# Attention in a two-layer trunk: pairs of heads in a pipeline of quarter query projections, with ScalarE normalising the probabilities

## The chip, the core and the metric

The kernel runs on one core of one Trainium2 chip. A core has five engines that work side by side, each through a list of instructions of its own, in order: TensorE (PE, matrix products and transposes, with its weight loads shown apart as PEld), VectorE (DVE), ScalarE (ACT), GpSimd (POOL) and SyncE (SP, which issues the transfers from memory here). An instruction at the head of its list waits until semaphores say that its inputs are there and its output buffer is free, and what stands behind it on that engine waits with it. PE writes to a small memory of eight banks called PSUM, from which DVE and ACT read. The metric is the device time of one execution in microseconds (us); lower is better.

## The reference

The program is a decoder trunk of two layers on 256 tokens of width 1024. Each layer is a feed-forward half step (SwiGLU, 2816 wide), a mixer, and a second half step, with RMSNorm before and after each. The mixer of layer 0 is a pooling; that of layer 1 is attention with 8 heads of width 64 in each of three groups (windows 128, 512, 2048 at dilations 1, 4, 16). Only that attention is touched:

```python
q = apply_rope((h @ w_q).reshape(B, S, 3, 8, 64), cos, sin)
for g, (window, dilation) in enumerate(ATTN_GROUPS):
    s = einsum(q[g], k[g]) * 64 ** -0.5          # masked to the window, causal, dilated
    m = max(s); p = exp(s - m); den = sum(p)
    o[g] = einsum(p / den, v[g]); lse[g] = m + log(den)
o = sum_g softmax(lse)[g] * o[g]
return o.reshape(B, S, 512) @ w_o
```

Since the three groups are joined by their softmax denominators, a head is one softmax over the keys of all three groups: exp over all of them, one sum, one division, and one product with the stacked values. Both kernels compute it so.

## The kernel before

The tokens are sorted by residue, so that for a tile of 128 tokens a head needs 512 keys: 256 of group 0, 128 of group 1, 128 of group 2. There are two token tiles (i = 0, 1) and four pairs of heads (pr = 0 to 3; heads 2 pr and 2 pr + 1).

Weights come in units of 128x1024 numbers (128x768 for the queries) by SyncE's queue. ACT makes the high part of each unit (a CAST, L92 or L100) and DVE the low part (a subtraction, L93 or L101), and PE forms every projection as three products of high and low parts. A unit's converted copy sits in one of eight buffers. The attention stage begins when the values have been projected (`vp`). For each pair there is a query projection `qp` of 24 matmuls per tile from four units, `rope` on DVE (L499, two of L502, L503), three transposes `qtp` (L611) and a copy `qT` on ACT (L612).

`scores(i, hd)` is for one head: three products into a bank `sc` (64 rows of PE's array, since a head is 64 wide), mask and maximum on DVE (L551), a factor on the maximum (`nm`, L553), and exp with its sum on ACT (L554). `values(i, hd)` transposes the 128x512 probabilities on PE (`ptp`, L564), copies them to SBUF on ACT (`pTt`, L567), and multiplies: the transposed probabilities are the stationary operand and the 64 columns of a head's values stream through, into 64 columns of a bank `ob`. `normed` divides a tile's result by the sums on DVE (L581, L583), transposes it (`otp`, L591) and splits it into high and low parts (`oT`, L593, L594). `o_proj` multiplies it with the output weights into `acc_o`.

Then comes a boundary, the object `go`: `go.first` is the norm after the mixer with the residual sum (`jk_pm`, L152, on ACT; `y_m` and `h` on DVE; a power on POOL), `go.second` the norm before the next half step (`jk_qm`, `n_m`), `go.third` the transposes `tp_m` (L181) and their split into `aT_m` (L183, L184). The next half step starts with 96 matmuls into `acc_b` (tile 0, then tile 1) and goes on with the gate `g`.

The order on each engine is found by a scheduler, which sorts the instructions when the program is built by their place in the text, by when they can run, and by which buffers are free. It has put the conversions of a pair's query units ahead of the work that waits for them, and interleaved the heads' work of tile 0 and tile 1 with the projections.

Of the kernel before, what the change touches and what calls it, by code (L numbers as in the profile page):

```python
# [47 lines left out]
def trunk_kernel(ctx: ExitStack, tc: tile.TileContext, x, pos, gains, pscale, ws, wq, invf, amask, pmat, icnt, out):  # L48
    nc = tc.nc

    cp = ctx.enter_context(tc.tile_pool(name="cp", bufs=1))
# [5 lines left out]
    sc4 = ctx.enter_context(tc.tile_pool(name="sc4", bufs=2))  # L57
    sc2 = ctx.enter_context(tc.tile_pool(name="sc2", bufs=7))
# [23 lines left out]
    last = {}  # L82
# [13 lines left out]
    def load_q_unit(u):  # L96
        raw = rawp.tile([P, 1024], F32, tag="raw", name=f"rawq{u}")
        nc.sync.dma_start(raw[:, :768], wq[u])
        hl = hlp.tile([P, 2, 1024], F32R, tag="hl", name=f"hlq{u}")
        nc.scalar.copy(hl[:, 0, :768], raw[:, :768])  # L100
        nc.vector.tensor_sub(hl[:, 1, :768], raw[:, :768], hl[:, 0, :768])  # L101
        return hl

    def mm(o, l, r, start, stop):
        nc.tensor.matmul(o, l, r, start=start, stop=stop)  # L105
# [102 lines left out]
    def acc_pair(name):  # L208
        return [accp.tile([P, 512], F32, tag="acc", name=f"acc_{name}{k}") for k in range(2)]
# [284 lines left out]
    def rope(src, i, nh, name):  # L494
        r = sc2.tile([P, nh, 2, 32], F32, tag="w2", name=f"ra_{name}")
        b = sc2.tile([P, nh, 2, 32], F32, tag="w2", name=f"rb_{name}")
        s4 = src.rearrange("p (h two d) -> p h two d", two=2, d=32)
        c4 = ctab[:, i : i + 1].to_broadcast([P, nh, 2, 32])
        nc.vector.tensor_mul(r, s4, c4)  # L499
        for z in range(2):  # L500
            sz = stab[:, i, z : z + 1].to_broadcast([P, nh, 32])
            nc.vector.tensor_mul(b[:, :, z], s4[:, :, 1 - z], sz)  # L502
        nc.vector.tensor_add(r, r, b)  # L503
        return r.rearrange("p h two d -> p (h two d)")
# [28 lines left out]
    den = [cp.tile([P, 8], F32, name=f"den{i}") for i in range(2)]  # L533
    ob = {}
    npt = [0]

    probs = {}

    def scores(i, hd, pool, tag):

        pr, off = hd // 2, (hd % 2) * 64
        q = qT[pr // 2][:, pr % 2]
        sc = pool.tile([P, 512], F32, tag=tag, name=f"sc{i}_{hd}")
        t = slice(i * P, (i + 1) * P)
        a = slice(off, off + 64)
        mm(sc[:, 0:256], q[a, 0, t], kT[0][a, pr, :], True, True)
        mm(sc[:, 256:384], q[a, 1, t], kT[1][a, pr, t], True, True)
        mm(sc[:, 384:512], q[a, 2, t], kT[2][a, pr, t], True, True)
        p = sc2.tile([P, 512], F32, tag="w2", name=f"p{i}_{hd}")
        mx = st.tile([P, 1], F32, tag="mx", name=f"mx{i}_{hd}")  # L550
        nc.vector.tensor_tensor_reduce(p, sc, am[:, i], 1.0, -3.0e38, op0=ALU.add, op1=ALU.max, accum_out=mx)  # L551
        nm = st.tile([P, 1], F32, tag="nm", name=f"nm{i}_{hd}")
        nc.vector.tensor_scalar_mul(nm, mx, -0.125)  # L553
        nc.scalar.activation(p, p, AF.Exp, bias=nm, scale=0.125, accum_out=den[i][:, hd : hd + 1])  # L554
        probs[i, hd] = p

    def values(i, hd):
        part, at = (0, hd * 64) if i == 0 else (hd // 4, (hd % 4) * 64)
        if (i, part) not in ob:
            ob[i, part] = accp.tile([P, 512], F32, tag="acc", name=f"ob{i}{part}")  # L560
        p = probs.pop((i, hd))
        tp = tpp.tile([P, 4, P], F32, tag="tp", name=f"ptp{i}_{hd}")
        for c in range(4):
            nc.tensor.transpose(tp[:, c], p[:, c * P : (c + 1) * P], ident)  # L564
        pT = pTt[:, npt[0] % 4]
        npt[0] += 1
        nc.scalar.copy(pT, tp)  # L567
        o = ob[i, part][:, at : at + 64]
        n = slice(hd * 64, hd * 64 + 64)
        mm(o, pT[:, 0], vt[0][:, 0, n], True, False)  # L570
        mm(o, pT[:, 1], vt[0][:, 1, n], False, False)
        mm(o, pT[:, 2], vt[1][:, i, n], False, False)
        mm(o, pT[:, 3], vt[2][:, i, n], False, True)

    acc_f = [None, None]

    def normed(i, part, heads):

        n = heads // 2
        rd = st.tile([P, 8], F32, tag="rd", bufs=2, name=f"rd{i}{part}")  # L580
        nc.vector.reciprocal(rd[:, :heads], den[i][:, part * heads : part * heads + heads])  # L581
        on = sc2.tile([P, heads, 64], F32, tag="w2", name=f"on{i}{part}")
        nc.vector.tensor_mul(  # L583
            on,
            ob[i, part][:, : heads * 64].rearrange("p (h d) -> p h d", d=64),
            rd[:, :heads].unsqueeze(2).to_broadcast([P, heads, 64]),
        )
        tp = tpp.tile([P, 4, P], F32, tag="tp", name=f"otp{i}{part}")
        onf = on.rearrange("p h d -> p (h d)")
        for c in range(n):  # L590
            nc.tensor.transpose(tp[:, c], onf[:, c * P : (c + 1) * P], ident)  # L591
        oT = sc4.tile([P, 2, n, P], F32R, tag="y", name=f"oT{i}{part}")
        nc.scalar.copy(oT[:, 0], tp[:, :n])  # L593
        nc.vector.tensor_sub(oT[:, 1], tp[:, :n], oT[:, 0])  # L594
        return oT

    def o_proj(i, oT, units, first, last):
        if first:
            acc_f[i] = acc_pair(f"o{i}")
        for k, u in enumerate(units):  # L600
            row_mm(acc_f[i], oT[:, 0, k], oT[:, 1, k], u, first and k == 0, last and k == len(units) - 1)

    for pr in range(4):
        units = [load_q_unit(pr * 4 + j) for j in range(4)]
        for i in range(2):
            ps = gup.tile([P, 512], F32, tag="gu", name=f"qp{pr}{i}")
            proj_mm(ps[:, :384], aT, i, units, 384)
            r = rope(ps[:, :384], i, 6, f"q{pr}{i}")
            tp = tpp.tile([P, 4, P], F32, tag="tp", name=f"qtp{pr}{i}")
            for c in range(3):  # L610
                nc.tensor.transpose(tp[:, c], r[:, c * P : (c + 1) * P], ident)  # L611
            nc.scalar.copy(qT[pr // 2][:, pr % 2, :, i * P : (i + 1) * P], tp[:, :3])  # L612
        for hd in (2 * pr, 2 * pr + 1):
            scores(0, hd, accp, "acc")
        if pr < 3:
            values(0, 2 * pr)
            values(0, 2 * pr + 1)
        if pr == 2:
            scores(1, 0, accp, "acc")
            scores(1, 1, accp, "acc")  # L620
            values(1, 0)
            values(1, 1)
    units = [load_unit() for _ in range(4)]
    scores(1, 2, gup, "gu")
    values(0, 6)
    scores(1, 3, gup, "gu")
    values(0, 7)
    scores(1, 4, gup, "gu")
    oT = normed(0, 0, 8)
    values(1, 2)  # L630
    scores(1, 5, gup, "gu")
    o_proj(0, oT, units, True, True)
    values(1, 3)
    scores(1, 6, gup, "gu")
    values(1, 4)
    scores(1, 7, gup, "gu")
    go.first(0, acc_f[0])
    oT = normed(1, 0, 4)
    values(1, 5)
    values(1, 6)  # L640
    go.second(0)
    o_proj(1, oT, units[:2], True, False)
    values(1, 7)
    go.third(0)
    oT = normed(1, 1, 4)
    o_proj(1, oT, units[2:], False, True)
    go(1, acc_f[1])

    aT = go.aT

# [113 lines left out]
```

## Time and profile before

| | before |
|---|---|
| median of 3 runs (lowest to highest) | 993.71 us (992.47 to 995.08) |
| the profiled execution | 995.63 us, of which its span is 993.7 |
| PE busy | 975.3 us, 98% of the span |
| DVE busy | 575.0 us, 58% |
| ACT busy | 484.4 us, 49% |
| first query matmul of the attention stage | 709.49 us into the span |
| first gate matmul of the half step behind it | 824.31 us |

Positions are in us from the start of the span. A row of a timeline gives the start, how long the run of instructions lasted, the engine, the line, and in brackets how long the engine had been idle and what ended that. A row of groups gives the count, the busy time of all together, the mean of one in nanoseconds, and the idle time ahead of them. `PEclk` is the share of its full clock that PE was granted. A run of matmuls overlaps with the next: from start to start is what one costs in a stream.

### The profile page before, as it was taken

What the parts mean: (1) busy time and instruction counts of PE and PEld (TensorE: products, weight loads), DVE (VectorE), ACT (ScalarE), POOL (GpSimd) and SP (SyncE); (2) the same over time, 40 slices, a digit from 0 to 9 for tenths busy, and PEclk for the clock granted to TensorE, in tenths of its full rate; (3) what the DMA queues carried; (4) which work ended last, traced back from release to release, by engine and by line L of the source; (5) the groups of instructions that cost most, each with busy time, mean ns of one, the idle gap of its engine ahead of it and who ended that gap; (6) DMA issues with size and microseconds to landing.
All of it is one profiled execution on the core that took longest, in us unless ns stands there. A gap on an engine that the chain in (4) does not pass through costs nothing.

```text
span 993.7 us, 12240 instructions
## 1 busy us (share of the span) xinstructions
PE 975.3 (98%) x4664; PEld 810.1 (82%) x4664; DVE 575.0 (58%) x725; ACT 484.4 (49%) x660; POOL 23.2 (2%) x34
## 2 busy tenths in 40 slices
PE   7999999999999999999999999999999999999997
PEld 6888888878788888877888888788898888888886
DVE  5665554578765555447665554685556466555542
ACT  5644443365564444346554443554455565444431
POOL 0000000010100000000000000100000000000000
PEclk8999999999999999999999999999999899999999
DMA  6855655666465575535755756474533137556531
GB/s 224 292 185 188 228 186 189 203 193 213 145 218 185 190 233 180 191 127 174 263 188 171 231 179 197 150 244 154 152 124 128 44 100 260 191 181 203 188 127 42
DMA packets 53722, 180.38 MB, mean 182 GB/s; under 512 B 7265, under 2 KB 7265, under 8 KB 53665
## 3 DMA queue, kind: packets, MB, share of 16 engines
q1 hardware_dynamic: 53584, 179.35, 55.4%
q8 instruction: 36, 0.59, 0.2%
q0 software_dynamic: 80, 0.26, 0.1%
q14 instruction: 22, 0.17, 0.1%
HBM read 178.54 MB, written 1.05 MB: 181 GB/s over the span
## 4 chain that ended last, share of the span: by engine, by line
PE 88%; DVE 4%; issue 3%; ACT 2%; POOL 2%; DMA 1%; SPq 0%; POOLq 0%; DVEq 0%; ACTq 0%
PE g L105 22%; PE acc_d L105 21%; PE acc_u L105 19%; PE acc_b L105 7%; PE vp L105 3%; PE qp L105 3%; PE kp L105 3%; PE htp L230 2%; PE ob L105 1%; PE acc_w L105 1%; PE acc_o L105 1%; DVE h L171 1%; DVE hl L93 1%; ACT hl L92 1%; PE sc L105 1%
## 5 line engine op out<-in xcount | busy, mean ns | idle before, releaser
L93 DVE TENSOR_TENSOR hl<-raw,hl 128x1024 fp32r<-128x1024 f32 x310 | 378.5, 1224 | 298.8 <-ACT hl L92 296.7
L92 ACT CAST hl<-raw 128x1024 fp32r<-128x1024 f32 x310 | 325.5, 1051 | 338.5 <-PE acc_d L105 101.1
L105 PE MATMUL acc_d<-hl,h 128*128 128x512 f32 x1056 | 242.9, 390 | 0.0
L105 PEld LDWEIGHTS acc_d<-hl,h 128*128 128x128 f32 x1056 | 197.4, 188 | 40.7
L105 PE MATMUL g<-hl,aT_m 128*128 128x512 f32 x480 | 116.1, 394 | 0.0
L105 PEld LDWEIGHTS g<-hl,aT_m 128*128 128x128 f32 x480 | 88.6, 188 | 17.8
L105 PE MATMUL acc_u<-hl,aT_m 128*128 128x512 f32 x384 | 88.3, 389 | 0.0
L105 PEld LDWEIGHTS acc_u<-hl,aT_m 128*128 128x128 f32 x384 | 72.1, 188 | 15.0
L105 PE MATMUL acc_u<-hl,aT_f 128*128 128x512 f32 x288 | 67.2, 390 | 0.0
L105 PEld LDWEIGHTS acc_u<-hl,aT_f 128*128 128x128 f32 x288 | 53.8, 188 | 11.5 <-DVE aT_f L184 0.5
L105 PE MATMUL g<-hl,aT_f 128*128 128x512 f32 x240 | 58.7, 395 | 0.0
L105 PE MATMUL g<-hl,aT_x 128*128 128x512 f32 x240 | 58.1, 394 | 0.0
L105 PEld LDWEIGHTS g<-hl,aT_x 128*128 128x128 f32 x240 | 44.3, 188 | 8.9
L105 PEld LDWEIGHTS g<-hl,aT_f 128*128 128x128 f32 x240 | 44.2, 188 | 8.7
L105 PE MATMUL acc_b<-hl,aT_m 128*128 128x512 f32 x192 | 45.3, 392 | 0.1
L105 PE MATMUL acc_u<-hl,aT_x 128*128 128x512 f32 x192 | 44.2, 389 | 0.0
L105 PEld LDWEIGHTS acc_u<-hl,aT_x 128*128 128x128 f32 x192 | 36.0, 188 | 7.5
L105 PEld LDWEIGHTS acc_b<-hl,aT_m 128*128 128x128 f32 x192 | 35.7, 188 | 7.8 <-DVE aT_m L184 0.5
L105 PE MATMUL qp<-hlq,aT_f 128*128 128x384 f32 x192 | 39.1, 346 | 0.0
L105 PE MATMUL kp<-hl,aT_hk 128*128 128x512 f32 x144 | 34.5, 394 | 0.0
L105 PEld LDWEIGHTS qp<-hlq,aT_f 128*128 128x128 f32 x192 | 32.7, 188 | 0.4
L105 PE MATMUL vp<-hl,aT_hk 128*128 128x512 f32 x144 | 33.1, 390 | 0.0
(158 smaller groups left out, 831.3 us busy)
## 6 DMA issues: line engine op xcount, KB each, us to landing
raw<-in_ws SPq DMA_DIRECT2D x310, 512.0 KB, 3.5
rawq<-in_wq SPq DMA_DIRECT2D x16, 384.0 KB, 3.6
gain_post<-in_gains SPq DMA_DIRECT2D x14, 256.0 KB, 4.6
gain_pre<-in_gains SPq DMA_DIRECT2D x12, 256.0 KB, 5.6
rawpm<-in_pmat SPq DMA_DIRECT2D x2, 512.0 KB, 4.7
out_dram<-h SPq DMA_DIRECT2D x4, 256.0 KB, 2.1
h<-in_x SPq DMA_DIRECT2D x2, 256.0 KB, 3.0
h<-in_x SPq DMA_DIRECT2D x1, 512.0 KB, 8.5
```

Source lines behind the costliest of these rows:

```text
L92: nc.scalar.copy(hl[:, 0, w], raw[:, w])
L93: last["dve"] = nc.vector.tensor_sub(hl[:, 1, w], raw[:, w], hl[:, 0, w])
L105: nc.tensor.matmul(o, l, r, start=start, stop=stop)
L171: nc.vector.scalar_tensor_tensor(h[i][:, c], y[:, c], rs, h[i][:, c], op0=ALU.mult, op1=ALU.add)
L230: nc.tensor.transpose(tp[:, k], prod[c, i][:, k * P : (k + 1) * P], ident)
```

## The change

Only the attention stage is rewritten. `scores(pr, i)` now does both heads of a pair: their products alternate between the lower and the upper 64 rows of PE's array, into two banks. `over_sums` takes the reciprocal of each head's sum on DVE (L560) and multiplies the head's 128x512 probabilities by it on ACT (L561); `normed` with its transposes is gone. `p_turn` transposes and copies the probabilities of a pair. `values` now has a head's values (64 columns) as the stationary operand and streams the transposed probabilities, so that the two heads write the lower and the upper 64 partitions of one bank, already in the layout that `o_proj` needs; ACT and DVE split that into `oT` (L588, L589). The query projection is cut into quarters (`q_proj`, 12 matmuls), and between the quarters stands the work of the pairs before. One query unit for the next pair is loaded and converted after each quarter (`next_q`). PE's order is fixed by the text for the whole stage, that of DVE and ACT for the loop over pairs; what stands behind the loop on DVE and ACT is left to the scheduler.

```diff
-        nc.scalar.activation(p, p, AF.Exp, bias=nm, scale=0.125, accum_out=den[i][:, hd : hd + 1])
-    def normed(i, part, heads):
...
+        for o, g, keys in ((0, 0, slice(0, S)), (256, 1, t), (384, 2, t)):
+            for e in range(2):
+                a = slice(e * 64, e * 64 + 64)
+                n = keys.stop - keys.start
+                mm(sc[e][:, o : o + n], q[a, g, t], kT[g][a, pr, keys], True, True)
...
+            den = st.tile([P, 1], F32, tag="den", name=f"den{i}_{pr}{e}")
+            nc.scalar.activation(p, p, AF.Exp, bias=nm, scale=0.125, accum_out=den)
+    def over_sums(pr, i):
+        for e, (p, den) in enumerate(probs[i, pr]):
+            rd = st.tile([P, 1], F32, tag="rd", name=f"rd{i}_{pr}{e}")
+            nc.vector.reciprocal(rd, den)
+            nc.scalar.mul(p, p, rd)
+            probs[i, pr][e] = p
...
+    def values(pr, i):
+        ob = gup.tile([P, 512], F32, tag="gu", name=f"ob{i}_{pr}")
+        for c, (g, j) in enumerate(((0, 0), (0, 1), (1, i), (2, i))):
+            for e in range(2):
+                n = slice((2 * pr + e) * 64, (2 * pr + e) * 64 + 64)
+                mm(ob[e * 64 : e * 64 + 64, 0:P], vt[g][:, j, n], pT[i, pr][e][:, c], c == 0, c == 3)
+        nc.scalar.copy(oT[i][:, 0, pr], ob[:, 0:P])
+        nc.vector.tensor_sub(oT[i][:, 1, pr], ob[:, 0:P], oT[i][:, 0, pr])
...
+    with tc.manual_schedule(engines={mybir.EngineType.PE}):
+        with tc.manual_schedule(engines={mybir.EngineType.DVE, mybir.EngineType.Activation}):
+            units += [load_q_unit(j) for j in range(4)]
+            for pr in range(4):
+                cur, units = units, []
+                q_proj(pr, 0, 0, cur)
+                if pr > 0:
+                    over_sums(pr - 1, 0)
+                    q_turn(pr - 1, 1)
+                if pr > 1:
+                    p_turn(pr - 2, 1)
+                next_q(pr, 0)
+                q_proj(pr, 0, 1, cur)
+                if pr > 0:
+                    scores(pr - 1, 1)
+                if pr > 1:
+                    values(pr - 2, 1)
+                if pr > 0:
+                    p_turn(pr - 1, 0)
+                next_q(pr, 1)
+                q_proj(pr, 1, 0, cur)
+                if pr > 0:
+                    over_sums(pr - 1, 1)
+                q_turn(pr, 0)
+                if pr > 0:
+                    values(pr - 1, 0)
+                next_q(pr, 2)
+                q_proj(pr, 1, 1, cur)
+                scores(pr, 0)
+                next_q(pr, 3)
+        o_proj(0, (0,))
+        over_sums(3, 0)
+        q_turn(3, 1)
+        o_proj(0, (1,))
+        scores(3, 1, gup, "gu")
+        o_proj(0, (2,))
+        p_turn(3, 0)
+        o_proj(1, (0,))
+        over_sums(3, 1)
+        values(3, 0)
+        p_turn(2, 1)
+        o_proj(0, (3,))
+        go.first(0, acc_f[0])
+        values(2, 1)
+        p_turn(3, 1)
+        o_proj(1, (1,))
+        go.second(0)
+        values(3, 1)
+        o_proj(1, (2, 3))
+    go.third(0)
+    go(1, acc_f[1])
```

How the instructions now stand shows at three places. In the names, `hlq10` is the converted query unit 10, `p0_10` the probabilities of tile 0, pair 1, head 0 of the pair, `rd` and `nm` the reciprocal and the factor that belong to it, `ptp1_00` the transposed probabilities of tile 1, pair 0, head 0, `qtp11` the transposed queries of pair 1, tile 1.

ACT in the middle of the loop, before: the conversions of the units for pair 3 and the work on pair 1 (there `p0_2` is tile 0, head 2).

```order
L100 CAST hlq12_5931<-rawq12_5929 128x768
L612 COPY qT0_5485<-qtp10_5675 128x3x128
L100 CAST hlq13_5936<-rawq13_5934 128x768
L100 CAST hlq14_5941<-rawq14_5939 128x768
L100 CAST hlq15_5946<-rawq15_5944 128x768
L554 ACTIVATE p0_2_5720,den0_5489<-p0_2_5720,nm0_2_5723 128x512
L612 COPY qT0_5485<-qtp11_5711 128x3x128
L567 COPY pTt_5488<-ptp0_2_5736 128x512
```

ACT at the corresponding place of the change, from the conversion of unit 10 to that of unit 12:

```order
L100 CAST hlq10_5746<-rawq10_5744 128x768
L554 ACTIVATE p0_10_5775,den0_10_5780<-p0_10_5775,nm0_10_5778 128x512
L554 ACTIVATE p0_11_5782,den0_11_5787<-p0_11_5782,nm0_11_5785 128x512
L100 CAST hlq11_5791<-rawq11_5789 128x768
L561 ACTIVATE p0_10_5775<-p0_10_5775,rd0_10_5807 128x512
L561 ACTIVATE p0_11_5782<-p0_11_5782,rd0_11_5810 128x512
L611 COPY qT0_5485<-qtp11_5813 128x3x128
L577 COPY pTt_5488<-ptp1_00_5818 128x512
L577 COPY pTt_5488<-ptp1_01_5824 128x512
L100 CAST hlq12_5832<-rawq12_5830 128x768
```

The conversions stood four together and well ahead of their use; now one stands after each quarter, behind the exps and the products of `over_sums`, and those stand behind it.

DVE in the change, at the same place and on into the next quarter:

```order
L101 TENSOR_TENSOR hlq11_5791<-rawq11_5789,hlq11_5791 128x768
L560 RECIPROCAL rd0_10_5807<-den0_10_5780 128x1
L560 RECIPROCAL rd0_11_5810<-den0_11_5787 128x1
L101 TENSOR_TENSOR hlq12_5832<-rawq12_5830,hlq12_5832 128x768
L499 TENSOR_TENSOR ra_q20_5847<-qp20_5794,ctab_261 128x384
L502 TENSOR_TENSOR rb_q20_5848<-qp20_5794,stab_262 128x6x32 x2
L503 TENSOR_TENSOR ra_q20_5847<-ra_q20_5847,rb_q20_5848 128x384
L550 ISA p1_10_5861,mx1_10_5862<-sc1_10_5853,qT0_5485 128x512
```

The low part of a unit stands ahead of the reciprocals in one quarter, and ahead of the rope and of the maxima in the next; each of them needs ACT's high part of that unit.

ACT at the boundary, in the change:

```order
L152 ACTIVATE jk_pm100_6293,ss_pm10_6292<-acc_o00_6184 128x512
L92 CAST hl247_6452<-raw247_6450 128x1024
L152 ACTIVATE jk_pm101_6295,ss_pm10_6292<-acc_o01_6185 128x512
L588 CAST oT1_5875<-ob1_2_6306 128x128
L577 COPY pTt_5488<-ptp1_30_6317 128x512
L577 COPY pTt_5488<-ptp1_31_6323 128x512
L92 CAST hl248_6457<-raw248_6455 128x1024
L92 CAST hl249_6462<-raw249_6460 128x1024
L152 ACTIVATE jk_qm100_6336,ss_qm10_6335<-h0_94 128x512
L588 CAST oT1_5875<-ob1_3_6349 128x128
L152 ACTIVATE jk_qm101_6338,ss_qm10_6335<-h0_94 128x512
L92 CAST hl250_6467<-raw250_6465 128x1024
```

Four conversions of units for the next half step now stand between the parts of tile 0's norms, where before they stood behind them or well ahead.

More of the change, by code (lines that the diff above doesn't have):

```diff
@@ L557, in values @@
[L557 to L573, printed above, removed]
@@ L575, in trunk_kernel @@
-    acc_f = [None, None]
-    def normed(i, part, heads):
[L579 to L595, printed above, removed]
@@ L597, in o_proj @@
-    def o_proj(i, oT, units, first, last):
-        if first:
-            acc_f[i] = acc_pair(f"o{i}")
[L600 to L642, printed above, removed]
@@ new lines, in over_sums, with p_turn @@
+    def over_sums(pr, i):
[4 more added lines that the diff above has]
+            probs[i, pr][e] = p
+    oT = [None, None]
+    pT = {}
+    def p_turn(pr, i):
+        pT[i, pr] = []
+        for e in range(2):
+            tp = tpp.tile([P, 4, P], F32, tag="tp", name=f"ptp{i}_{pr}{e}")
+            for c in range(4):
+                nc.tensor.transpose(tp[:, c], probs[i, pr][e][:, c * P : (c + 1) * P], ident)
+            pT[i, pr].append(pTt[:, npt[0] % 4])
+            npt[0] += 1
+            nc.scalar.copy(pT[i, pr][e], tp)
@@ L644, in trunk_kernel @@
     go.third(0)
-    oT = normed(1, 1, 4)
-    o_proj(1, oT, units[2:], False, True)
     go(1, acc_f[1])
+    aT = go.aT
     aT = go.aT
```

48 lines of the change are left out of this document (32 added, 16 removed).

## The prediction

> **What bounds the kernel now.** I read first the page's busy times, then the timeline of PE through the attention stage, then busy time and clock by stretch.
>
> ```profile
> PE 975.3 (98%) x4664; PEld 810.1 (82%) x4664; DVE 575.0 (58%) x725; ACT 484.4 (49%) x660; POOL 23.2 (2%) x34
> ```
>
> ```profile
> 709.49 6.43 PE L105 MATMUL qp<-hlq,aT_f 128*128 128x384 f32 x36
> 715.76 0.49 PE L611 MATMUL qtp<-ident,ra_q 128*128 128x128 f32 x3
> 716.01 2.33 PE L105 MATMUL qp<-hlq,aT_f 128*128 128x384 f32 x12
> 718.27 1.68 PE L105 MATMUL sc<-kv,qT 64*128 64x256 f32 x12
> 719.88 1.84 PE L105 MATMUL qp<-hlq,aT_f 128*128 128x384 f32 x9
> ...
> 725.22 1.00 PE L105 MATMUL ob<-kv,pTt 128*128 128x64 f32 x8
> 726.03 0.60 PE L105 MATMUL qp<-hlq,aT_f 128*128 128x384 f32 x2
> ...
> 764.87 2.22 PE L105 MATMUL sc<-kv,qT 64*128 64x256 f32 x18
> ...
> 803.21 8.33 PE L105 MATMUL acc_b<-hl,aT_m 128*128 128x512 f32 x36
> 811.37 1.04 PE L181 MATMUL tp_m<-ident,n_m 128*128 128x128 f32 x8
> ...
> 824.31 2.89 PE L105 MATMUL g<-hl,aT_m 128*128 128x512 f32 x12
> ```
>
> ```profile
> 720.00:733.40 13.40, 13.40 (x90) 12.81 (x90) 8.03 (x19) 7.52 (x13) 0.00 (x0) 1.00 0.38 121
> 733.40:750.00 16.60, 16.33 (x106) 14.25 (x105) 11.04 (x29) 9.13 (x16) 0.00 (x0) 1.00 0.45 157
> 782.00:790.00 8.00, 7.04 (x42) 5.85 (x40) 6.12 (x15) 5.62 (x15) 1.43 (x2) 0.79 0.00 1
> 790.00:798.00 8.00, 7.25 (x41) 6.37 (x42) 2.59 (x3) 3.65 (x5) 0.00 (x0) 0.79 0.20 63
> 798.00:803.20 5.20, 5.20 (x28) 4.20 (x27) 1.98 (x5) 2.04 (x4) 0.00 (x0) 1.00 0.30 108
> ```
>
> PE bounds it: 98% of the span. The stage runs from 709.49 to the first gate matmul at 824.31, 114.8 us, and I use two marks inside: the last scores of tile 0 (764.87, 55.4 us after the start), and the end of the last `acc_o` (803.2, 93.7 us). From 720 to 750 PE is busy 29.7 of 30.0 us, ACT 16.7 and DVE 19.1: the two others have slack because their work is spread out ahead of PE. Only from 782 to 798 does PE wait, and there the clock column reads 0.79: 0.21 of 16 us is 3.4 us, which is 6.8 us at half clock.
>
> From start to start a query matmul costs 6.27/36 = 0.174 us, the scores of two heads 1.61, a head's eight value products 0.81, an `acc_b` (or `acc_o`) matmul 8.16/36 = 0.227.
>
> **The change part by part.**
>
> *PE.* Removed are 8 transposes, under 1 us. The two heads of a pair may overlap on PE: at worst they cost what they do now, at best half (8 x 1.61 and 16 x 0.81 us, so up to 13 us of PE work less). The trace holds no product into 64 columns, so both ends stay. I take the middle, but it matters only where PE is the engine that is waited for. One pass of the loop asks of PE, at the prices above, 48 x 0.174 = 8.4 for queries, 2 x 1.61 for scores, 4 x 0.81 for values, and 22 transposes of about 0.11 (`qtp`: three in 0.25 from 715.76 to 716.01 gives under that), in all about 17.3 us, and down to 14 if all overlaps.
>
> *ACT and DVE in the loop.* Here lies the main term. Rows for what stands in the chain:
>
> ```profile
> L100 ACT CAST hlq<-rawq 128x768 fp32r<-128x768 f32 x16 | 13.4, 837 | 11.1 <-PE qp L105 7.4 <-PE vp L105 3.6
> L101 DVE TENSOR_TENSOR hlq<-rawq,hlq 128x768 fp32r<-128x768 f32 x16 | 15.3, 958 | 16.0 <-ACT hlq L100 15.8
> L551 DVE CUSTOM_DVE_ANT_0 p<-sc,qT 128x512 f32<-128x512 f32 x16 | 10.8, 685 | 0.8 <-PE sc L105 0.8
> L551 DVE DVE_READ_ACCUMULATOR2_ANT mx<- 128x1 f32 x16 | 1.3, 83 | 0.0
> L553 DVE TENSOR_SCALAR nm<-mx 128x1 f32<-128x1 f32 x16 | 2.3, 147 | 0.0
> L581 DVE RECIPROCAL rd<-den 128x4 f32<-128x4 f32 (+1 forms) x3 | 0.5, 182 | 0.5 <-ACT p L554 0.5
> L197 ACT ACTIVATE n_f<-n_f,rs_qf 128x512 f32<-128x512 f32 x6 | 4.3, 722 | 7.3 <-POOL rs_qf L156 7.3
> L612 ACT COPY qT<-qtp 128x384 f32<-128x384 f32 x8 | 3.8, 470 | 0.0
> ```
>
> ```profile
> 713.88 0.56 DVE L499 TENSOR_TENSOR ra_q<-qp,ctab 128x384 f32<-128x384 f32 x1 [1.87 <-PE qp L105]
> 714.35 0.61 DVE L502 TENSOR_TENSOR rb_q<-qp,stab 128x192 f32<-128x192 f32 x2
> 715.00 0.56 DVE L503 TENSOR_TENSOR ra_q<-ra_q,rb_q 128x384 f32<-128x384 f32 x1
> ...
> 721.33 0.72 ACT L554 ACTIVATE p<-p,nm 128x512 f32<-128x512 f32 x1 [0.82 <-DVE nm L553]
> 721.96 0.19 ACT L554 ACTIVATION_READ_ACCUMULATOR p<-p,nm 128x1 f32 x1
> 722.08 0.48 ACT L612 COPY qT<-qtp 128x384 f32<-128x384 f32 x1
> ...
> 782.98 1.06 ACT L567 COPY pTt<-ptp 128x512 f32<-128x512 f32 x2
> ```
>
> In the fixed order ACT and DVE hand to each other in a ring. Take the half pass from the conversion of unit 10 to that of unit 12: high part on ACT 0.84; low part on DVE 0.96; the rope behind it 1.68 (713.88 to 715.56); maximum and its read 0.77; factor 0.15; an exp with its read 0.75 (721.33 to 722.08), the second 0.75; high part of unit 11 0.84; its low part 0.96; the reciprocals behind that 0.18; two products 0.72 each (L197, the same kind of instruction); query copy 0.47; two probability copies 1.06. The sum is 10.9 us. Neighbours on one engine start about 0.1 before the one ahead has ended (721.96 plus 0.19 against 722.08), which takes off some 0.7; seven hand-overs at about 0.04 (721.30 to 721.33) give 0.3 back. That makes 10.5 us, and the other half pass, with the small `oT` cast in it, the same. None of these steps waits for PE: the rope's projection and the transposes are ready before their turn. So a pass takes 21 us against PE's 17.3 or less, and PE, with its own fixed order, waits: before `values`, whose copies end the ring's half (about 2 us a pass), before scores (0.8), and for units 7 and 11 (1).
>
> For the whole loop: 8.9 us of PE work before the first scores (51 instructions of 0.174 or less); about 18.3 for the first full pass, which has no pair behind it and so two copies and one cast less; 21.2; and 22.2 for the last, whose units are larger (1.05 and 1.22 against 0.84 and 0.96). The last scores of tile 0 start at 70.6, against 55.4 now: **15.2 us later**. The cover that is lost is the four conversions done together ahead of need.
>
> *The tail to the last `acc_o`.* Now 93.7 - 55.4 = 38.3 us. The change has left for it two heads' scores, three pairs of value products, the `ptp` of three pairs and all 48 output matmuls: 48 x 0.227 + 2 x 1.61 + 6 x 0.81 + 27 x 0.11 = 21.9, or 19.6 where pairs overlap. To that come waits. The first `acc_o` needs the bank of the last query projection, free after its rope, which stands behind the low part of unit 18 on DVE, whose high part ACT starts only after the last query copy: 1.05 + 1.22 + 1.68 less 1.3 of scores, 2.7 us. Values of pair 3 wait 1.5 for copies behind the exps, and 0.7 falls elsewhere. Sum 24.5, **13.8 less than now**; the last `acc_o` ends at 95.1 against 93.7.
>
> *The boundary.* Now it hides nearly all: tile 0's norm is over before the last `acc_o`, and seven `acc_b` matmuls and eight transposes are done by then; from 803.2 to 824.31 are 21.1 us. In the change tile 0 finishes its output products 8 us before the end, and its norms have four conversions of 1.05 between them:
>
> ```profile
> 781.67 0.60 ACT L152 ACTIVATE jk_pm<-acc_o 128x512 bf16<-128x512 f32 x1 [4.29 <-PE acc_o L105]
> ...
> 789.10 0.72 ACT L197 ACTIVATE n_m<-n_m,rs_qm 128x512 f32<-128x512 f32 x1 [0.97 <-POOL rs_qm L156]
> ```
>
> That chain takes 8.15 us now (781.67 to 789.82), though two exps and three copies stand in it. With the conversions and the other tile's norm in ACT's order I count 9.7, so PE stands 2.0 us before `tp_m`, then 1.8 for the two copies before the first `acc_b`. With 7 x 0.227 and 0.9 of transposes that had been done already, the boundary takes 27.6: **6.5 more**. If the conversions slipped in without delay it would be 5.
>
> *The clock.* In the row 782 to 790 PE was busy 7.04 of 8 us and its clock was halved for 6.8 us all the same, so stretches with gaps of this size can bring that on. The change has such gaps in each pass and at the boundary. In the loop the ring has about 4 us a pass to spare, and a slow PE hides there; at the boundary nothing hides it. I count one such spell in full, **3.4 us more**; none and three are the ends, 0 and 10.
> The Trainium skill (TensorE: Matmul & The Clock Gate, Part 1) says that the clock falls to half when PE is idle for a window of about 3.4 us, and that gaps above about 3 us should be avoided. This case's spell came with busy time missing in pieces, so the row is stricter; by the rule alone no gap here is long enough, and the sum would end 3.4 lower, which is the second case below.
>
> *Sum.* 15.2 - 13.8 + 6.5 + 3.4 = 11.3 us. The profiled execution, 995.63 with a span of 993.7, would become 1006.9; it lies 1.9 above the median of the runs, 993.71, so the forecast is **1005.0 us**.
>
> **The rivals.**
>
> (a) *The ring, with no slow clock.* All as above, and the gaps stay harmless: 993.7 + 7.9 = 1001.6. For it: most gaps I found are 2 us or less.
> (b) *More slow spells.* Three of them in full, or pairs that do not overlap on PE together with two: 1009 and above. For it: PE would be used in only 17 of 21 us in the loop.
> (c) *PE stays the bound.* If the ring were shorter than PE's work, because conversions run ahead of their place or the products are cheaper than L197, the stage costs what PE needs: about 81 us to the last `acc_o` with pairs at the old price and 4 of waits, 85 for 93.7, the boundary still 1 or so dearer: 993.7 - 8 = 986. This is the other sign, and it decides once a half pass falls under 8.7 us, half of 17.3. Against it: the order is fixed, and the sum of durations alone is above that by 1.8 us even with overlaps taken off. The Trainium skill (TensorEngine Tiling (Array Packing), Key Properties) has tiles working independently, which would help this case, and a drain at each change of tiling mode, which would cost it.
> (d) *It comes out even.* A half pass near 9 us and a boundary that hides: 993.7 within 3 us.
>
> **How the numbers follow.** Forecast 0.46, (a) 0.25, (b) 0.13, (c) 0.10, (d) 0.06. The first three are slower by more than 0.3% (3 us, about what a measurement of this kernel tells from no change): 0.84; same 0.06; faster 0.10. The range 996 to 1012 takes in (a), the forecast and most of (b), and reaches down towards (d); (c) lies outside it. The forecast's own range is 1002 to 1009.
>
> **What would show it.** Right: in the loop DVE's idle time ahead of L499 and L101 is ended by ACT, ACT's ahead of L554 and L561 by DVE, each a few us a pass; PE waits for `pTt` before `ob`; passes of 21 us between scores of tile 0; scores of pair 3, tile 0 some 70 us after the first query matmul; a gap of 2 us before `tp_m`; a clock under 1 in the stage. Wrong: PE busy without gaps in the loop, passes of 17 us or less, or `acc_b` starting within 1 us of the last `acc_o`.

## The result, and the profile after

The changed kernel takes **1003.92 us** (median of 4 runs, 1002.71 to 1004.07) against 993.09 for the kernel before on the same chip: ratio **1.0109**, 95% interval 1.0095 to 1.0123. It is slower by 10.8 us, as forecast (1005.0, range 996 to 1012). The profiled execution took 1004.07 us with a span of 1002.3.

| stretch (us) | before | predicted | after |
|---|---|---|---|
| first query matmul to last scores of tile 0 | 55.4 | 70.6 | 70.6 |
| from there to the end of the last `acc_o` | 38.3 | 24.5 | 23.4 |
| from there to the first gate matmul | 21.1 | 27.6, and 3.4 for the clock | 29.8 |
| the stage | 114.8 | 126.1 | 123.8 |

The busy times of the engines have hardly moved: PE does 6 us less, ACT 8 us more.

```profile
PE 968.9 (97%) x4656; PEld 799.1 (80%) x4656; DVE 576.1 (57%) x740; ACT 492.1 (49%) x681; POOL 24.6 (2%) x34
```

The timeline of PE through the stage, after (start, duration, engine, line, operation; in brackets the idle time ahead and what ended it):

```profile
708.99 6.43 PE L105 MATMUL qp<-hlq,aT_f 128*128 128x384 f32 x36
...
717.79 1.15 PE L105 MATMUL sc<-kv,qT 64*128 64x256 f32 x12
...
735.96 1.15 PE L105 MATMUL sc<-kv,qT 64*128 64x256 f32 x12 [0.22 <-ACT qT L611]
...
742.61 0.44 PE L105 MATMUL qp<-hlq,aT_f 128*128 128x384 f32 x1 [0.63 <-ACT hlq L100]
743.61 1.15 PE L105 MATMUL qp<-hlq,aT_f 128*128 128x384 f32 x5 [0.55 <-DVE hlq L101]
745.47 1.15 PE L105 MATMUL sc<-kv,qT 64*128 64x256 f32 x12 [0.72 <-ACT qT L611]
...
752.84 1.57 PE L105 MATMUL ob<-pTt,kv 128*64 128x128 f32 x16 [1.76 <-ACT pTt L577]
...
756.91 1.15 PE L105 MATMUL sc<-kv,qT 64*128 64x256 f32 x12 [0.22 <-ACT qT L611]
...
774.27 1.98 PE L105 MATMUL ob<-pTt,kv 128*64 128x128 f32 x16 [2.23 <-ACT pTt L577]
...
779.61 1.15 PE L105 MATMUL sc<-kv,qT 64*128 64x256 f32 x12
...
782.29 1.40 PE L105 MATMUL acc_o<-hl,oT 128*128 128x512 f32 x5 [1.11 <-DVE rb_q L502]
...
799.85 3.13 PE L105 MATMUL acc_o<-hl,oT 128*128 128x512 f32 x12
805.38 1.35 PE L181 MATMUL tp_m<-ident,n_m 128*128 128x128 f32 x8 [2.40 <-DVE n_m L195]
807.51 8.02 PE L105 MATMUL acc_b<-hl,aT_m 128*128 128x512 f32 x23 [0.79 <-ACT aT_m L183]
...
832.81 2.43 PE L105 MATMUL g<-hl,aT_m 128*128 128x512 f32 x10
```

PE, which hardly ever stood still in the loop before, now waits in every pass: for the conversions of a unit (0.63 and 0.55), for the query copy (0.72) and for the copies of the probabilities (1.76). The scores of tile 0 start at 717.79, 735.96, 756.91 and 779.61: passes of 18.2, 20.9 and 22.7 us.

One half pass on ACT, from the conversion of unit 10 to that of unit 12:

```profile
735.97 0.84 ACT L100 CAST hlq<-rawq 128x768 fp32r<-128x768 f32 x1
740.23 0.72 ACT L554 ACTIVATE p<-p,nm 128x512 f32<-128x512 f32 x1 [3.42 <-DVE nm L552]
...
741.74 0.82 ACT L100 CAST hlq<-rawq 128x768 fp32r<-128x768 f32 x1
743.72 1.34 ACT L561 ACTIVATE p<-p,rd 128x512 f32<-128x512 f32 x2 [1.16 <-DVE rd L560]
744.96 0.46 ACT L611 COPY qT<-qtp 128x384 f32<-128x384 f32 x1
745.32 1.07 ACT L577 COPY pTt<-ptp 128x512 f32<-128x512 f32 x2
746.28 0.85 ACT L100 CAST hlq<-rawq 128x768 fp32r<-128x768 f32 x1
```

And DVE in the same stretch:

```profile
736.84 0.96 DVE L101 TENSOR_TENSOR hlq<-rawq,hlq 128x768 fp32r<-128x768 f32 x1 [0.44 <-ACT hlq L100]
737.72 0.55 DVE L499 TENSOR_TENSOR ra_q<-qp,ctab 128x384 f32<-128x384 f32 x1
...
742.59 0.96 DVE L101 TENSOR_TENSOR hlq<-rawq,hlq 128x768 fp32r<-128x768 f32 x1 [1.60 <-ACT hlq L100]
743.47 0.22 DVE L560 RECIPROCAL rd<-den 128x1 f32<-128x1 f32 x2
```

Read the two together. ACT converts (735.97), then stands idle for 3.42 us because DVE does the low part, the rope (from 737.72) and the maximum one behind the other; DVE then stands idle for 1.60 until ACT has done two exps and the next conversion; ACT waits again for 1.16 until the low part and the reciprocals are done. Both engines are idle in turn and neither waits for PE. From conversion to conversion it is 746.28 - 735.97 = 10.3 us, and the other half pass, to the conversion at 756.92, is 10.6.

### The profile page after: what moved, and what is told of

Its sections match the earlier page's. It is cut to its first block, busy times and chain, and to the rows that moved or that the text cites. A ratio compares the mean times of both kernels' runs of the same rounds, so it can differ in the third digit from the quotient of the medians.

```text
span 1002.3 us, 12237 instructions
## 1 busy us (share of the span) xinstructions
PE 968.9 (97%) x4656; PEld 799.1 (80%) x4656; DVE 576.1 (57%) x740; ACT 492.1 (49%) x681; POOL 24.6 (2%) x34
## 4 chain that ended last, share of the span: by engine, by line
PE 80%; DVE 7%; ACT 6%; issue 4%; POOL 2%; DMA 1%; SPq 0%; POOLq 0%; DVEq 0%; ACTq 0%
PE g L105 22%; PE acc_d L105 21%; PE acc_u L105 19%; PE acc_b L105 7%; PE vp L105 3%; PE kp L105 3%; PE htp L230 2%; ACT hl L92 1%; DVE hl L93 1%; PE acc_w L105 1%; DVE h L171 1%; ACT p L554 1%; POOL rs_qf L156 1%; ACT hlq L100 1%; ACT p L561 1%
## 5 line engine op out<-in xcount | busy, mean ns | idle before, releaser
L105 PE MATMUL acc_b<-hl,aT_m 128*128 128x512 f32 x192 | 47.4, 407 | 0.9 <-ACT aT_m L183 0.8
```

## The experiments

All times are medians, beside 992.5 to 993.1 for the kernel before in the same sittings; a difference between sittings is known to about that 0.6 us. Experiments 9 and 10 ran on another chip than 1 to 8. Theory 1 is the prediction's: a ring in which ACT and DVE hand to each other sets the passes of the loop. Its rivals put the length of a pass down to PE's own fixed order (theory 2) or to the amount of work on ACT (theory 3).

### 1. The low parts later

The conversion's second half, on DVE, is cut off from the first and put one quarter later, behind the rope and the maxima, or behind the reciprocals.

```diff
-        units.append(load_q_unit(pr * 4 + 4 + k) if pr < 3 else load_unit())
...
+        nc.scalar.copy(hl[:, 0, :n], raw[:, :n])
+        high.append((hl, raw, n))
...
+    def low():
+        if high:
+            hl, raw, n = high.pop(0)
+            last["dve"] = nc.vector.tensor_sub(hl[:, 1, :n], raw[:, :n], hl[:, 0, :n])
...
                     over_sums(pr - 1, 0)
+                    low()
...
                     scores(pr - 1, 1)
+                low()
```

and the same behind `over_sums(pr - 1, 1)` and `scores(pr, 0)`, and once behind the loop.

> The changed kernel with one thing moved: the low part of each unit that is converted in the loop (DVE) is put one quarter later in DVE's order, behind the rope, the maxima and the reciprocals instead of ahead of them. ACT's order, PE's order and all work stay. Theory 1 (the ring of ACT and DVE): the link from ACT's high part to the rope and the reciprocals is cut, so a half pass no longer takes 10.5 us; the passes fall from 21 to what PE needs, 15 to 17, the last scores of tile 0 start 57 to 60 us after the first query matmul instead of 70.6, and the time falls by 10 to 14 us, to 990 to 994. Theory 2 (PE's fixed order and the latencies from projection over rope to scores set the pass): passes stay near 21, time within 1 us of the change's 1004. Theory 3 (ACT has too much work): the work is the same, within 1 us.

Measured: **987.27 us** (986.19 to 987.69), 16.7 less than the change and 0.9942 of the kernel before (0.9927 to 0.9957). PE's timeline there:

```profile
748.97 1.15 PE L105 MATMUL sc<-kv,qT 64*128 64x256 f32 x12
...
764.92 1.15 PE L105 MATMUL sc<-kv,qT 64*128 64x256 f32 x12
...
771.73 1.15 PE L105 MATMUL sc<-kv,qT 64*128 64x256 f32 x12 [2.36 <-ACT qT L611]
```

The passes are 15.95 us without a wait ahead of the scores, and the last scores of tile 0 start 56.3 us after the first query matmul (708.62 there). The same instructions on the same engines, with one link cut: theories 2 and 3 fall. The time fell by more than expected, since the boundary became shorter too (24.7 us in place of 29.8), though it was not edited: only two conversions stood in tile 0's norm now, and no slow clock followed. The tail, on the other hand, took 25.2 us, 1.8 more than in the change: the gap of 2.36 in the last row and a slow clock behind it. Experiments 6 and 8 take these up.

### 2. Without the products

> The changed kernel without the 16 products with the reciprocals on ACT (the division by the sums is left out, so the output is not the reference's; the reciprocals stay). Theory 1 (ring): a half pass loses the two products (1.34 us) and also the wait for the low part and the reciprocals ahead of them (0.96 + 0.2), since the query copy no longer stands behind them: 10.5 - 2.5 = 8.0, below PE's need, so passes of 15 to 17 us, last scores of tile 0 at 57 to 60, time 990 to 994. Theory 3 (ACT's work): only the 1.34 of a half pass go, passes of 18.3, last scores near 62.5, time near 996. Theory 2 (PE's order): passes stay near 21, time 1002 to 1004.

```diff
             nc.vector.reciprocal(rd, den)
-            nc.scalar.mul(p, p, rd)
```

The division by the sums is left out, so this is a test of the time alone. Measured: **989.59 us** (987.88 to 990.78), 14.3 less than the change; passes of 15.6, 16.7 and 17.1. ACT from conversion to conversion, in this kernel:

```profile
740.33 0.85 ACT L100 CAST hlq<-rawq 128x768 fp32r<-128x768 f32 x1
...
748.73 0.84 ACT L100 CAST hlq<-rawq 128x768 fp32r<-128x768 f32 x1
```

A half pass is 8.4 us, 1.9 to 2.2 less than in the change: more than the 1.34 of the two products themselves, since the wait for the reciprocals went with them. One thing was expected wrongly: 8.4 is not below what PE needs. Experiment 1 shows that to be 15.95 a pass, 8.0 a half pass, so the ring still sets the pace here by a little.

### 3 and 4. The same idle copies at two places

Two copies on ACT into a scratch buffer, ahead of a conversion or behind it, in every second quarter. The one line moves by one place.

```diff
+    def idle_copy(pr, k):
+        if k in (0, 2) and pr > 0:
+            for z in range(2):
+                jk = sc1.tile([P, 512], BF16, tag="junk", bufs=1, name=f"jx{pr}{k}{z}")
+                nc.scalar.copy(jk, kT[0][:, 0:2])
...
+        idle_copy(pr, k)                         # experiment 3
         units.append(load_q_unit(pr * 4 + 4 + k) if pr < 3 else load_unit())
+        idle_copy(pr, k)                         # experiment 4, in place of the other
```

> The changed kernel with two idle copies on ACT (128x512 into a scratch buffer, about 1 us together) added in quarters 1 and 3 of passes 2 to 4, just ahead of the high part of the unit. Theory 1 (ring): that place is in the ring, so each of the six pairs delays the next exps in full: passes of 23, last scores of tile 0 at 75.5 to 76.6, time 5 to 6 us above the change's 1004. Theory 2 (PE's order): no change, within 1 us. Theory 3 (ACT's work): some us more, as much as in the kernel where the same copies stand one place later.

> The same six pairs of idle copies on ACT one place later, just behind the high part of the unit, where ACT stands idle for 3.4 us before the exps. Theory 1 (ring): there the ring has left ACT for DVE (low part, rope, maximum), so 1 us more of ACT work costs nothing: passes of 21, last scores at 70.6, time within 1 us of the change's 1004. Theory 2: no change either. Theory 3 (ACT's work): as much as with the copies one place earlier, some 5 us.

Measured: **1011.36 us** ahead (1009.93 to 1011.82), **1003.44** behind (1002.56 to 1004.59), against 1003.92 for the change. ACT with the copies (L620) ahead of the conversion:

```profile
748.33 1.28 ACT L620 CAST jx<-kv 128x512 bf16<-128x512 f32 x2
...
753.77 0.72 ACT L554 ACTIVATE p<-p,nm 128x512 f32<-128x512 f32 x1 [3.41 <-DVE nm L552]
```

and behind it:

```profile
746.37 1.28 ACT L620 CAST jx<-kv 128x512 bf16<-128x512 f32 x2
749.90 0.72 ACT L554 ACTIVATE p<-p,nm 128x512 f32<-128x512 f32 x1 [2.25 <-DVE nm L552]
```

Ahead, ACT's wait for DVE is as long as ever, and everything behind is later by 1.2 us. Behind, the wait takes the copies in: 2.25 in place of 3.41. The last scores of tile 0 start 76.5 us after the first query matmul ahead (785.17 less 708.72), and 69.8 behind (778.18 less 708.36), against 70.6 in the change. Five of the six pairs stand ahead of those scores: 5 x 1.18 = 5.9, and 5.8 is measured. That is the plainest proof of the ring: one and the same 1.2 us of ACT work costs all of itself or nothing, by whether the ring runs through ACT at that moment. (That experiment 4 is 0.8 faster is no gain of the copies. Its first two passes are those of the change, 18.2 and 20.9; the last is 21.9 in place of 22.7, since the slow clock comes earlier in it, where PE had a wait to lose: 0.60 ahead of the values in place of 2.23.) The profiled execution of experiment 3, the shortest of its four, has 5.8 us more span than that of the change: 5.8 in the loop and 1.2 in the tail, where the sixth pair stands, less 0.9 at the boundary, where the slow clock lasted for a shorter time. The medians lie 7.4 apart, and no trace shows where the other runs have their last 1.5.

### 5. DVE and ACT in the scheduler's order

```diff
-        with tc.manual_schedule(engines={mybir.EngineType.DVE, mybir.EngineType.Activation}):
+        if True:
```

> The changed kernel with the order of DVE and ACT in the loop left to the scheduler; PE's order and all work stay as in the change. If the fixed order of the two engines makes the passes long (the ring), passes of 15 to 18 us, last scores of tile 0 at 57 to 63 us after the first query matmul, and 985 to 998 us. If PE's fixed order, or the work itself, sets the pass, 1002 or more with passes near 21.

Measured: **982.46 us** (981.13 to 983.08), ratio 0.9902 to the kernel before (0.9887 to 0.9916): the fastest of all, better than expected and better than both kernels. Busy time in its loop (the stretch and its length, then the busy time of PE, PEld, DVE and ACT, and the clock third from the end):

```profile
718.12:764.58 46.46, 45.28 (x355) 40.89 (x355) 30.94 (x88) 35.35 (x69) 0.00 (x0) 1.00 0.38 123
```

From the first scores to the last of tile 0 PE is busy 45.28 of 46.46 us, at full clock throughout. The scheduler has put the conversions of a pass together again, four in a run on ACT (3.90 us for the 1024-wide ones) ahead of need. So the fixed order of the two engines alone costs 1003.92 - 982.46 = 21.5 us, and without it the rest of the change is worth 10 us. In the traces the loop is shorter by 15.4 us (55.3 in place of 70.6), the tail by 1.7 and the boundary by 5.2: the order in the loop also settles how many conversions are left for tile 0's norm, two here and four in the change.

### 6. Tile 0's norm without conversions in it

On the changed kernel, the units 4 to 8 of the next half step are held back on ACT and DVE.

```diff
     go.third(0)
+    hold.update(act=last["t_act"].ins, dve=last["t_dve"].ins, units=range(unit_no[0] + 3, unit_no[0] + 8))
...
+            with held("act", u):          # queued behind tile 0's aT_m
                 nc.scalar.copy(hl[:, 0, w], raw[:, w])
```

> The changed kernel with the conversions of units 4 to 8 of the next half step held back on ACT and DVE until tile 0's aT_m is written; before they stood inside tile 0's norms. The loop stays. If these conversions make tile 0's norm late: from the start of jk_pm to tp_m 7 to 8 us instead of 10.1, the gap of 2.4 us ahead of tp_m and most of the 0.8 behind it go, and with the gap the spell of half clock behind it (3.0 us); 998 to 1001 us. If the norm is as long without them, or the slow clock comes from elsewhere: within 1.5 us of 1004. What could give part of it back: units 4 to 8 now come late for the first acc_b matmuls, up to 1.5 us.

Measured: **1000.31 us** (999.82 to 1001.12), 3.6 less. In its timelines (ACT, then PE; `tp_m` is L188 there):

```profile
795.87 0.60 ACT L159 ACTIVATE jk_pm<-acc_o 128x512 bf16<-128x512 f32 x1
```

```profile
803.33 1.03 PE L188 MATMUL tp_m<-ident,n_m 128*128 128x128 f32 x8
805.29 0.74 PE L112 MATMUL acc_b<-hl,aT_m 128*128 128x512 f32 x2 [0.93 <-ACT aT_m L190]
```

From `jk_pm` to `tp_m` it is 7.5 us, and `tp_m` no longer waits; in the change it was 10.1 (795.25 to 805.38). The wait of 0.93 ahead of `acc_b` stayed. The 31 `acc_b` matmuls that follow run at full clock, at about 0.24 each: the slow spell is gone with the gap. The boundary takes 25.6 us (803.50 to 829.09) in place of 29.8. About 2.6 of gap and 2.9 of slow clock have gone, and some 1.2 has come back in short waits around the first `acc_b` matmuls. So the conversions in the chain account for 4.2 of the 8.7 us by which the boundary had grown over the kernel before, about half of it directly and half through the clock. Of the rest, 2.5 is work that the kernel before had done ahead of the last `acc_o`, and 0.9 the wait ahead of `acc_b`.

### 7 and 10. Heads one after the other

What is it worth that the two heads of a pair alternate on PE? The two loops are turned round, in the kernel of experiment 1 and in that of experiment 5:

```diff
-        for o, g, keys in (...):
-            for e in range(2):
+        for e in range(2):
+            for o, g, keys in (...):          # the same in values
```

> The kernel with the low parts later (987.3 us), in which PE sets the pass; now the two heads of a pair do their scores and their value products one head after the other instead of by turns. If the low price of a pair (1.08 us for scores, 1.02 for values, against 1.61 and 1.62 for two heads in the kernel before) comes from the two heads overlapping on PE, it goes back to the old prices: 8 x 0.53 + 8 x 0.6 = 9 us more PE work, of which 6 to 9 show, 993 to 997 us. If it comes from the shape of the products alone, the order of the matmuls does not matter: within 1 us of 987.

> The kernel with the free order of DVE and ACT (982.5 us), with the two heads of a pair one after the other in scores and values instead of by turns. In the fixed order with the low parts later the same edit made scores 4.8 and values 3.0 us dearer, and 4.0 us of it showed. If the difference was hidden there behind PE's waits (3.3 us in the stage), here with 2 us of waits 6 to 8 us show: 988 to 990.5. If the turns are worth only 4 us wherever PE sets the pass: 986 to 987.

Measured: **991.27 us** (990.39 to 991.87) on experiment 1's 987.27, and **988.35** (988.19 to 988.71) on experiment 5's 982.46. A pair's scores, its values and what follows on PE, first in experiment 5 (by turns), then in experiment 7 (one after the other):

```profile
739.69 1.15 PE L105 MATMUL sc<-kv,qT 64*128 64x256 f32 x12
740.76 1.09 PE L105 MATMUL ob<-pTt,kv 128*64 128x128 f32 x16
741.79 1.09 PE L574 MATMUL ptp<-ident,p 128*128 128x128 f32 x8
```

```profile
741.35 1.68 PE L105 MATMUL sc<-kv,qT 64*128 64x256 f32 x12
742.96 1.58 PE L105 MATMUL ob<-pTt,kv 128*64 128x128 f32 x16
744.47 1.09 PE L574 MATMUL ptp<-ident,p 128*128 128x128 f32 x8
```

From start to start a pair's scores cost 1.07 us by turns and 1.61 one after the other, which is the price in the kernel before; its values cost 1.03 by turns and 1.51 one after the other, against 1.62 in the kernel before. So the turns are worth 8 x 0.54 = 4.3 us for the scores and 8 x 0.48 = 3.8 for the values, and that the values are now the stationary operand is worth little by itself, 8 x 0.11 = 0.9. Of these 8.2 us of the turns 4.0 show in experiment 7, less than the 6 to 9 expected. In experiment 10 it is 5.9, and its 988.35 lies in the range expected. Waits of PE take part of it in: those that the rows show fall from 4.0 us in the stage to 2.7, and from 2.1 to 1.3. Shorter ones inside the rows take in more (12 `qp` last 2.76 us in a row of experiment 1 and 2.35 in that of experiment 7), but the difference was not followed to the last microsecond.

### 8. Experiment 1 with the query copy first and the norm unbroken

> The kernel with the low parts later (987.3 us), with two more moves: the last query transposes and their copy stand ahead of the products with the reciprocals and of the last conversion on ACT, and units 4 to 8 of the next half step are converted behind tile 0's aT_m. The gap of 2.4 us ahead of the last scores of tile 1 and the half clock behind it (1.7 us) should go: 982 to 985 us. If PE only stands later, at the values of pair 3 or at the first acc_b matmuls, 986 to 988.

```diff
+                if pr == 3:
+                    o_proj(0, (0,))
+                    q_turn(3, 1)
                 next_q(pr, 3)
             low()
-        o_proj(0, (0,))
         over_sums(3, 0)
-        q_turn(3, 1)
```

with the lines of experiment 6. Measured: **985.11 us** (984.68 to 985.77), 2.2 less than experiment 1 and at the edge of the two expectations. In PE's timeline the gap of 2.36 ahead of the last scores has gone:

```profile
771.46 1.15 PE L112 MATMUL sc<-kv,qT 64*128 64x256 f32 x12 [0.19 <-ACT qT L618]
...
777.90 1.09 PE L112 MATMUL ob<-pTt,kv 128*64 128x128 f32 x14 [0.75 <-ACT pTt L584]
```

and with it the slow clock behind it; but PE then waits 0.75 in the middle of the values of pair 3. The gain is all in the tail, which takes 22.0 us in place of 25.2. The boundary takes 25.6, 0.9 more than in experiment 1, so holding the conversions back brings nothing here: in experiment 1 `tp_m` did not wait for the norm any more. An order written by hand comes within 2.7 us of the scheduler's, and does not reach it.

### 9. The free order without the products

The edit of experiment 2 on the kernel of experiment 5.

> The kernel with the free order of DVE and ACT (982.5 us) without the 16 products with the reciprocals on ACT (the division by the sums is left out, the output is not the reference's). In the fixed order leaving them out took 14.3 us. If they cost that much only because they stand in the ring, here, where PE sets the pass, they are free: 981 to 983 us, and PE's remaining waits of some 2 us in the stage are the most that can go. If ScalarE's products are a cost of their own, wherever they stand: 16 x 0.67 = 10.7 us of ACT work less, of which several us show, 972 to 979.

Measured: **980.98 us** (980.72 to 982.46), 1.5 less. Most of that is one wait of 1.18 us ahead of the second scores, which the trace of experiment 5 has and this one has not. The same 10.7 us of ACT work are worth 14.3 us in the ring and 1.5 outside it. That ScalarE normalises the probabilities is not what makes the change slow.

## Why the prediction came out right, point by point

**The bound, and the ring.** Right, in its place and its size. A half pass was put at 10.5 us and took 10.3 and 10.6. The passes were put at 18.3, 21.2 and 22.2 and took 18.2, 20.9 and 22.7, the last with a slow spell in it. PE's waits were put at 2 ahead of the values, 0.8 ahead of the scores and 1 for a unit; they were 1.6 to 2.2, 0.7 and 1.2. The last scores of tile 0 start 70.6 us after the first query matmul, as forecast. That this agrees to the tenth is in part luck: the ring by itself gives 69.8, as experiment 4 shows, and 0.8 came from a slow clock that the prediction let hide there. The reason given for the short first pass is also only half of it. Two copies and a cast less are 1.3 us of the 2.9; the rest is that the first scores start 1.6 us after a conversion on ACT (717.79 against 716.16) and the later ones together with it (735.96 and 735.97). Experiments 1 to 5 show the cause. What made it predictable is that each step had its duration in the trace of before and the order told what stands behind what.

**PE's own work.** The prediction left open whether pairs overlap (17.3 us a pass if not, 14 if fully) and took the middle; experiment 1 has 15.95. The price of a pair's scores is 1.08 us against 1.61, a third less and not half; the value products came down from 1.62 to 1.02. Since PE was not what was waited for, this moved nothing in the change, as the prediction said it would not. It did set rival (c): "PE stays the bound" was priced at 986, and the kernel in which it is so takes 982.5. The point from which it decides was put at a half pass of 8.7 us and is 8.0.

**The tail.** 24.5 forecast, 23.4 measured. The bank of the last query projection came free sooner: PE waited 1.1 us ahead of `acc_o` and not 2.7. The row of that wait names L502 as what ended it, so the bank is free before the rope's last addition, which the prediction had counted, and PE reached that matmul later than assumed. Pair 3's values waited 1.2, against 1.5. The waits come to 2.3 us and not 4.9, but PE's own work came to 21.1 and not 19.6 (a low end that the prediction gives without its sum): two errors that partly cancel.

**The boundary and the clock.** 27.6 (its parts add up to 27.4) and 3.4 forecast, 29.8 measured. The gap ahead of `tp_m` was put at 2.0 and was 2.4, since the chain of the norm takes 10.1 and not 9.7; the one ahead of `acc_b` at 1.8 and was 0.8, since `acc_b` began at 807.51, as soon as the first of the two copies to `aT_m` was done. The slow spell came where it was expected: the row of 23 `acc_b` matmuls lasts 8.0 us, and at 0.227 from start to start it would be about 5.4; with 0.3 for `tp_m` that is 2.9. A second spell fell into the last pass, where the prediction let it hide behind the ring; the scores behind it show no wait, so PE was the one waited for there, and by experiment 4's last pass 0.8 us of it came through. Experiment 6 shows the cause of the gap. The spell follows the gap in each kernel that kept it (2.25 to 2.43 us in experiments 2, 3 and 4, with 7.0 to 8.0 us for the 23 `acc_b` matmuls) and is missing in those that did not.

**The sum.** This is where two errors met. The stage was to grow by 11.3 us and grew by 9.0 (the span by 8.6, as the stage starts 0.5 earlier): tail and boundary were each about 1.1 too dear. The profiled execution of before, on which the sum was made, lies 2.5 us above the median of all runs of that kernel (993.09), more than the 1.9 taken off; that of the change lies at its median. So 8.6 in the spans is 10.8 in the medians, and the forecast of 1005.0 is nearer to 1003.9 than its parts deserve. The terms that were mis-sized are named above; none was of the wrong sign.

**The rivals.** (a), the ring without a slow clock at 1001.6, is refuted by the spell at the boundary; (b), three spells or more, did not come in the change but came in experiment 3; (c) and (d) needed a half pass of 9 us or less, and it was 10.3. The drain that (c) weighs against the working in parallel is not separated by any run here.

## What to carry to other kernels

When an order is fixed by hand on two engines that feed each other, write down one round with the duration of each step and what it stands behind: if the steps of both engines form one chain, its length is the pass, however idle either engine is on average. Work that depends on nothing near it (here the conversions) should stand where an engine would otherwise be idle, and its two halves on two engines should not stand directly behind one another. Test such a chain by moving an idle instruction by one place: it costs all of itself or nothing.

## What the runs showed of the hardware

PE's clock fell to half without any stretch in which PE was idle for long. Busy time and granted clock in pieces of 3.4 us (behind the length stands PE's busy time; the third number from the end is the clock), of the change:

```profile
721.60:725.00 3.40, 2.60 (x12) 1.70 (x10) 1.09 (x3) 2.24 (x5) 0.00 (x0) 1.00 0.07 9
725.00:728.40 3.40, 2.74 (x25) 2.58 (x26) 2.00 (x5) 1.34 (x3) 0.00 (x0) 1.00 0.39 113
...
751.40:754.80 3.40, 1.91 (x19) 1.50 (x19) 1.05 (x2) 2.60 (x6) 0.00 (x0) 1.00 0.02 5
754.80:758.20 3.40, 3.18 (x24) 2.70 (x24) 1.02 (x5) 2.60 (x5) 0.00 (x0) 1.00 0.46 154
...
771.90:775.30 3.40, 1.11 (x14) 0.74 (x14) 1.09 (x5) 3.33 (x8) 0.00 (x0) 1.00 0.12 47
775.30:778.70 3.40, 3.40 (x17) 3.07 (x13) 1.36 (x3) 1.98 (x5) 0.00 (x0) 0.50 0.23 52
...
806.00:812.80 6.80, 6.01 (x18) 4.45 (x16) 6.16 (x11) 3.67 (x9) 2.01 (x2) 0.50 0.24 74
```

of experiment 4, which has at the place of the first two rows the same three short gaps (0.18, 0.55 and 0.72 us):

```profile
721.60:725.00 3.40, 1.98 (x9) 1.06 (x7) 1.09 (x3) 2.24 (x5) 0.00 (x0) 1.00 0.26 42
725.00:728.40 3.40, 3.38 (x19) 2.98 (x20) 2.63 (x6) 1.84 (x3) 0.00 (x0) 0.50 0.39 121
```

and of the kernel before:

```profile
783.20:786.60 3.40, 2.52 (x21) 2.21 (x20) 3.00 (x8) 2.21 (x7) 0.56 (x1) 1.00 0.01 2
786.60:793.40 6.80, 6.72 (x25) 5.64 (x24) 2.33 (x6) 3.22 (x8) 0.86 (x1) 0.50 0.00 0
```

Each spell lasts 3.4 or 6.8 us. The gaps of 2.23 and 2.40 us of the change were each followed by one, the gap of 1.76 was not; the three short gaps were followed by one in experiment 4 and by none in the change. PE had been busy for 1.98 us of the piece ahead of a spell in experiment 4, for 2.52 in the kernel before, and for 1.91 in the change at a place where no spell came. So neither the longest gap nor the busy time of such a piece decides alone; what does stays open. The Trainium skill (TensorE: Matmul & The Clock Gate, Part 1) describes a free-running window of 3413 ns and the half rate as what follows an idle one. The length of the spells agrees with that window; but no piece of that length ahead of a spell here was idle, so an idle window is not what brought these spells on. Where a gap was taken away (at the boundary in experiment 6, ahead of the last scores in experiment 8) the spell behind it went too.

Two heads by turns on different halves of PE's rows or columns overlap in part: a pair costs a third less, for scores (1.61 to 1.07 us) as for values (1.51 to 1.03), and not half; the Trainium skill (TensorEngine Tiling (Array Packing), Key Properties) says that different tiles can load and multiply in parallel, with which the direction agrees.
